# Order of the product pairs, queue of the gate stores, spread of the first loads and buffers of branch B's results in a hybrid mLSTM and differential-attention block

## Chip, cores and metric

One Trainium2 chip, one core of it. The metric is the device time of one execution in microseconds (us), less is better. Time before: median 1725.19 us of three runs (1722.07 to 1732.42).

## The reference, cut to what matters

S = D = 1024, batch 1, one layer, float32. The input is normalised, projected by `w_in` into twelve segments, and goes through two branches: A is an mLSTM with four heads of 256 in both directions over chunks of 128, behind a convolution of width five on its q and k; B is differential attention with eight heads (two score maps of 64 channels each, values of 128). Both results are projected, weighed with sigmoid gates, added, projected again and added to the input.

```python
h = rmsnorm(x, norm_g[layer])
proj = jnp.einsum('bsd,de->bse', h, w_in[layer])
(a_q, a_k, a_v, a_o, a_z, a_g, b_q, b_k, b_v, b_z, g_a, g_b) = jnp.split(
    proj, _split_points(), axis=-1)
...
hm = rmsnorm((h_fw + h_bw).transpose(0, 2, 1, 3), ml_norm_g[layer])
...
y_a = hm * jax.nn.sigmoid(a_o) * jax.nn.silu(a_z)
...
att = diff_attention(dq, dk, da_v, lam)
...
y_b = att.reshape(B, S, DA_WIDTH).astype(x.dtype) * jax.nn.silu(b_z)
...
mix = (jax.nn.sigmoid(g_a + gb[0]) * jnp.einsum('bsc,cd->bsd', y_a, w_branch_a[layer])
       + jax.nn.sigmoid(g_b + gb[1]) * jnp.einsum('bsc,cd->bsd', y_b, w_branch_b[layer]))
x = x + jnp.einsum('bsd,de->bse', mix, w_out[layer])
```

## The kernel before, in words

Every float32 product is made of three products in a rounded float32 form: each operand is split into a high part H and the low rest L, and H·H, L·H and H·L are added in PSUM. ScalarE casts the high parts, VectorE or GpSimd (POOL) subtracts for the low ones.

The program is a list of small units, each a few matmuls with what belongs to them, put in order by hand in `build` (L1572). `add` appends units; `weave` mixes two lists by their costs and by when a unit can be ready, so that one list fills the gaps of another. The order of TensorE (PE) is the order of this list (`keep(E.PE)`, L1671). The other engines, SyncE (SP) with its DMA queue among them, get their order from a scheduler that works with modelled times. Every engine executes in order: an instruction that waits holds back all behind it.

The stages, with their times in the profile:

1. Opening, 0 to 68 us: norm, transposes of the input, first z projections.
2. Product pairs, 68 to 490: the branch A segments of `w_in`. Two blocks of 128 columns are handled as a pair and multiplied in seven products in place of eight. `pairs` (L1617 on) lists sixteen narrow pairs (the pairs of k, q, o and z; `pair_units` L335, matmuls of 128x512 at L356) and then two wide pairs, the values (`wide_units` L375, seven products of 48 matmuls of 128x256 at L401). Within a pair the products run in the order 0, 3, 1, 4, 2, and 6 and 5 come interleaved with the next pair. The weight form of a product is made by `load_form` (L294) or `load_wide_form` (L258): sums or differences of the raw weight pieces on POOL (L264, L279), the cast on ScalarE (L287), the low part on VectorE for products 0, 4 and 6 and on POOL for the others (L288). A wide pair has four raw pieces of 128x4x256. Two go to `raw` tiles with the pair (`load_piece`, L246), and the two far ones to slots of the tag `big` (`kit`, six slots which the narrow pairs' results use too), through `spare` and `far_pieces`, called inside the last narrow pair's units (L1687 and L1688 of `build`). The sinks of the pairs convolve (L500 to L512), apply o and z, or store the values (L436).
3. Differential attention, 490 to 1148: per head and per block of queries scores (L1069), exponentials (L1074), transposes (L132), products with the values (L1105). Between them gate projections (`gate_units`, L960), the next heads' q, k and z projections (L558, L580) and values (`da_v`, L1038) serve as filler. `da_v(0)`, the values of heads 0 and 1, runs wholly ahead of head 0.
4. mLSTM, 1148 to 1425: `ml_units` (L1383) writes the order. For head n: `k` (L1186, L1225) and `v` (L1205) load and weigh chunks, `gb` (L1197) loads gate rows for the weight matrices W (L1280, L1282), `HL` (L1192) loads split k and q, `state` updates the matrix memories, `S` starts the scores. Nine gate projections are filler. A gate's `done` (L964) runs tanh on ScalarE into the tile `gt`, which has one buffer, and stores it (L967).
5. Rest of the gates and the passes through the branches' weights, 1425 to 1630: `load_y` (L1453) loads 128x1024 rows of a branch result into `yraw` (L1455, two buffers), casts on ScalarE (L1457), subtracts on VectorE (L1458). Branch B's eight (`yb`) come first.
6. Output projection and last norm, 1630 to 1724. The output weights (L1509) and squares (L1548) use the tag `yraw` too.

Of the kernel before, what the change touches and what calls it, by code (L numbers as in the profile page):

```python
# [7 lines left out]
F32 = mybir.dt.float32  # L8
# [6 lines left out]
S = 1024  # L15
D = 1024
# [4 lines left out]
NC = S // L  # L21
# [89 lines left out]
class Block:  # L111
# [110 lines left out]
    def pair_raws(self, p):  # L222
# [25 lines left out]
    def spare(self, n):  # L248
        while len(self.kit) < n:
            self.kit.append(self.big("kit")[:, 0:S])  # L250

    def far_pieces(self, p, blocks=(1, 0)):
        i = 0 if p % 2 == 0 else 4
        for b in blocks:
            self.praws[p][b][1] = self.kit[i + 1 - b].rearrange("p (k e) -> p k e", e=256)
            self.load_piece(p, b, 1)

    def load_wide_form(self, key):  # L258
        _, p, f = key
        a, g = self.a, self.p  # L260
        self.pair_raws(p)
        r1, r2 = self.praws[p]
# [697 lines left out]
    def gate_units(self, seg, i):  # L960
# [3 lines left out]
        def done(half, ps):  # L964
            t = self.wpool.tile([128, 512], F32, name="gt", tag="gt")
            self.a.activation(out=t, in_=ps, func=AF.Tanh, scale=0.5, bias=self.gbh[:, idx:idx + 1])  # L966
            (self.a if self.opening else self.q).dma_start(out=self.tg[seg][i][:, half * 512:(half + 1) * 512], in_=t)  # L967
# [415 lines left out]
    def ml_units(self, heads, gates):  # L1383
# [6 lines left out]
        for c in (3, 2, 1, 0):  # L1390
            un += x["k"](c) + x["v"](c)
        for c in range(NC):
            un += x["gb"](c) + x["HL"](c)
        un += take(8) + x["weigh"](3, 1) + take(3) + x["state"](3, 1)
        un += x["weigh"](2, 1) + take(5) + x["state"](2, 1)
        un += x["weigh"](1, 1) + take(4) + x["state"](1, 1) + x["split"](0)
        un += take(4) + x["S"](0)
        prev = None
        for n, x in enumerate(heads):
# [5 lines left out]
            for t in range(8):  # L1405
# [35 lines left out]
                if prev and t in (0, 2):  # L1441
                    un += prev["g"](t // 2)
                if nx:
# [9 lines left out]
    def load_y(self, src, i, slot):  # L1453
        raw = self.wy.tile([128, S], F32, name="yraw", tag="yraw", bufs=2)
# [45 lines left out]
    def load_wo(self, k, st, which):  # L1500
# [5 lines left out]
        else:  # L1506
            raw = self.wy.tile([128, D], F32, name="yraw", tag="yraw", bufs=2)
# [7 lines left out]
    def out_units(self, st):  # L1515
# [14 lines left out]
        def piece(t, i, g):  # L1530
# [16 lines left out]
            sq = self.wy.tile([128, D], F32, name="sqo", tag="yraw", bufs=2)  # L1547
# [24 lines left out]
    def build(self):  # L1572
# [21 lines left out]
        with pool(name="const", bufs=1) as self.const, \  # L1594
# [22 lines left out]
            self.pairs, sinks, self.praws, self.f, self.kit = [], [], {}, {}, []  # L1617
            for n in range(NH_A):
# [54 lines left out]
            w.add(do(lambda: setattr(self, "opening", False)), leave("p0"), enter("s0", "s0", side="right"), *g3)  # L1673
# [11 lines left out]
            fv = self.first_v  # L1685
# [13 lines left out]
            w.add(do(lambda: setattr(self, "ahead", True)), *qk[0], *z[0], *self.da_v(0, sts[0:2]))  # L1699
            prev = None  # L1700
            for h in range(NH_B):
# [7 lines left out]
                else:  # L1709
                    nxt = z[h - 1] + ahead + fill(FILL[h]) + z[h] if h else ahead + fill(FILL[0])  # L1710
# [82 lines left out]
```

## Time and profile before

| what | value |
|---|---|
| median of three runs | 1725.19 us (1722.07 to 1732.42) |
| profiled execution, its own time | 1725.98 us |
| its span in the trace | 1724.2 us |
| mean granted TensorE clock | 0.984 |
| busy: PE, VectorE (DVE), ScalarE (ACT), POOL | 1653.9, 1015.4, 776.8, 661.2 us |
| bytes on SP's and ACT's hardware queue | 196.03 MB |

The span leaves out 1.8 us of the profiled execution's time, before its first and behind its last recorded instruction. In the views, a row of the waits names the waiting instruction, its releaser, the total, the number of times and the longest; a row of the timeline has start, duration, engine, line, operation, output and inputs, and in brackets the idle time ahead of it with what ended it; a row of the windows has the stretch, its length, the busy time of each engine with the number of instructions, the granted clock, the share of the DMA engines and GB/s. SPq is SP as it issues DMAs; the time beside it is the issue, not the transfer.

### The profile page before, as it was taken

Reading aid. Unit: us, or ns where it says so; the run is one execution under the profiler, and the core shown is the slowest. Engines: PE = TensorE matmul, PEld = TensorE weight load, DVE = VectorE, ACT = ScalarE, POOL = GpSimd, SP = SyncE. Lnnn points to the kernel's source line nnn. Section 1 sums busy time; section 2 is a strip of 40 time slices with the busy share of each in tenths; the row PEclk is TensorE's granted clock in tenths of the full one; section 3 lists DMA queues with packets and bytes.
Section 4 is the critical chain, followed back from the end, with each engine's and each line's share of the span. In section 5 each row is a group of like instructions: output and inputs, shape, how many; then the busy total and the mean of one; then the engine's idle time right before and its main releaser. Section 6 shows DMA issues by size and latency. Waiting matters only on the chain. (4 is left out here: it accounts for less than half of the span.)

```text
span 1724.2 us, 25403 instructions
## 1 busy us (share of the span) xinstructions
PE 1653.9 (96%) x9335; PEld 1385.9 (80%) x9335; DVE 1015.4 (59%) x1817; ACT 776.8 (45%) x1548; POOL 661.2 (38%) x713
## 2 busy tenths in 40 slices
PE   7999999997999999999999999996999998999998
PEld 6777887877988788878878887785988876888887
DVE  5687678773324866777676676512666663226533
ACT  6455555553322545554554545523566653122221
POOL 4767766665342452533435152122232221222000
PEclk9999999998999999999999999998999998999999
DMA  5343434344252313212132231148777527444222
GB/s 182 94 134 115 147 110 135 110 153 128 111 172 61 86 37 86 70 38 79 48 88 54 58 86 38 50 144 227 225 217 201 154 81 243 134 145 136 86 86 86
DMA packets 191248, 199.77 MB, mean 116 GB/s; under 512 B 13466, under 2 KB 144883, under 8 KB 191123
## 3 DMA queue, kind: packets, MB, share of 16 engines
q1 hardware_dynamic: 189922, 196.03, 37.7%
q10 hardware_dynamic: 1200, 2.11, 0.3%
q8 instruction: 73, 1.20, 0.3%
q14 instruction: 53, 0.43, 0.1%
HBM read 124.60 MB, written 56.72 MB: 105 GB/s over the span
## 5 line engine op out<-in xcount | busy, mean ns | idle before, releaser
L558 PE MATMUL pj<-hH,wH 128*128 128x512 f32 x640 | 270.0, 422 | 13.9 <-ACT gt L966 11.9
L558 PE MATMUL pj<-hH,wL 128*128 128x512 f32 x640 | 253.3, 396 | 1.4 <-POOL wL L210 1.4
L558 PE MATMUL pj<-hL,wH 128*128 128x512 f32 x640 | 252.5, 394 | 0.0
L1074 ACT ACTIVATE e<-S,nm 128x1024 f32<-128x1024 f32 x128 | 142.5, 1115 | 98.0 <-DVE nm L1072 97.9
L212 POOL TENSOR_TENSOR wL<-raw,wH 128x1024 fp32r<-128x1024 f32 x34 | 82.7, 2433 | 235.4 <-ACT wH L207 235.4
L558 PEld LDWEIGHTS pj<-hH,wH 128*128 128x128 f32 x640 | 122.3, 191 | 47.3 <-issue 14.6
L1072 DVE TENSOR_REDUCE nm<-S 128x1 f32<-128x1024 f32 x128 | 150.6, 1218 | 13.6 <-PE S L1069 13.0
L558 PEld LDWEIGHTS pj<-hH,wL 128*128 128x128 f32 x640 | 121.5, 190 | 30.7 <-POOL wL L210 3.2
L558 PEld LDWEIGHTS pj<-hL,wH 128*128 128x128 f32 x640 | 122.2, 191 | 17.2 <-DVE hL L709 0.2
L558 PE MATMUL pj<-sl_yb,wH 128*128 128x512 f32 x384 | 122.1, 397 | 6.8 <-ACT sl_yb L1457 4.7
L1094 DVE TENSOR_TENSOR pL<-T,pH 128x512 fp32r<-128x512 f32 x128 | 87.2, 688 | 70.0 <-ACT pH L1093 68.6
L1093 ACT CAST pH<-T 128x512 fp32r<-128x512 f32 x128 | 75.1, 587 | 79.9 <-PE T L132 78.3
L1069 PE MATMUL S<-kst,qq 64*128 64x512 f32 x768 | 107.9, 411 | 1.7 <-ACT e L1074 1.7
L207 ACT CAST wH<-raw 128x1024 fp32r<-128x1024 f32 x48 | 50.4, 1051 | 107.0 <-PE pj L558 89.8
L558 PEld LDWEIGHTS pj<-sl_yb,wH 128*128 128x128 f32 x384 | 73.2, 191 | 25.8 <-ACT sl_yb L1457 6.2
L1080 DVE SCALAR_TENSOR_TENSOR e<-e,r,e 128x1024 f32<-128x1024 f32 x64 | 91.2, 1425 | 2.2
L1069 PEld LDWEIGHTS S<-kst,qq 64*128 64x128 f32 x768 | 68.5, 186 | 27.1 <-issue 11.4
L356 PE MATMUL T<-TH,wH 128*128 128x512 f32 x256 | 86.9, 398 | 1.1 <-ACT u L363 1.1
L502 DVE SCALAR_TENSOR_TENSOR pj<-cin,cols,pj 128x512 f32<-128x512 f32 x128 | 87.1, 747 | 1.1 <-ACT pj L500 1.1
L356 PE MATMUL T<-TH,wL 128*128 128x512 f32 x256 | 86.2, 398 | 1.4 <-ACT u L363 1.1
L132 PE MATMUL T<-ident,e 128*128 128x128 f32 x512 | 77.0, 273 | 5.4 <-ACT att L1107 3.5
L580 PE MATMUL pj<-wH,hH 128*128 128x256 f32 x256 | 75.8, 296 | 3.1 <-DVE hl L1002 2.2
(398 smaller groups left out, 4414.8 us busy)
## 6 DMA issues: line engine op xcount, KB each, us to landing
raw<-in_w_in_dram SPq DMA_DIRECT2D x84, 512.0 KB, 4.2
kst<-hl SPq DMA_DIRECT2D x64, 128.0 KB, 2.4
qq<-hl SPq DMA_DIRECT2D x64, 128.0 KB, 2.4
x<-in_x_dram SPq DMA_DIRECT2D x8, 512.0 KB, 6.4
cak<-y SPq DMA_DIRECT2D x16, 256.0 KB, 2.3
cakH<-cin SPq DMA_DIRECT2D x16, 256.0 KB, 4.4
cakL<-tz SPq DMA_DIRECT2D x16, 256.0 KB, 4.5
gm<-oz SPq DMA_DIRECT2D x16, 256.0 KB, 2.6
```

Source lines behind the costliest of these rows:

```text
L132: self.t.transpose(out, in_, self.ident[0:k, 0:k])
L212: self.p.tensor_tensor(out=wL, in0=raw, in1=wHf, op=ALU.subtract)
L356: self.t.matmul(ps, lhsT=l[:, k, :], rhs=r[:, k, :], start=(first and k == 0 and m == 0), stop=(k == 3 and m == 2), skip_group_check=not f ...
L502: v.scalar_tensor_tensor(out=acc, in0=raw[:, o + x:o + x + 512], scalar=w(x), in1=acc, op0=ALU.mult, op1=ALU.add)
L558: self.t.matmul(ps, lhsT=l[:, k, :], rhs=r, start=(n == 0), stop=(n == 23))
L580: self.t.matmul(ps[:, i, :], lhsT=l, rhs=r[:, k, :], start=(kh == 0 and k == 0 and m == 0), stop=(kh == 1 and k == 3 and m == 2))
L1069: self.t.matmul(ps[:, o], lhsT=qq[r, x, c], rhs=k[r, y, o], start=(m == 0), stop=(m == 2))
L1072: v.tensor_reduce(out=nm, in_=ps, axis=AX.X, op=ALU.max, negate=True)
L1074: a.activation(out=e, in_=ps, func=AF.Exp, bias=nm[:, 0:1], accum_out=Z[:, j, t:t + 1])
L1080: v.scalar_tensor_tensor(out=e0, in0=e, scalar=r[:, 0:1], in1=e0, op0=ALU.mult, op1=ALU.add)
L1093: a.copy(pH[:, :, s], ps)
L1094: v.tensor_tensor(out=pL[:, :, s], in0=ps, in1=pH[:, :, s].bitcast(F32), op=ALU.subtract)
```

## The change

1. The wide pairs are the first two of `pairs`. All six slots of `big` are allocated as `kit` as soon as the pool exists, all four pieces of a wide pair are loaded at once, and both pairs' pieces with the first form. `spare` and `far_pieces` are gone.
2. While the flag `ml` is set (stage 4), a gate's store is issued by ScalarE, which made the tile, and not by SP. 19 stores move, 13 stay.
3. The first mLSTM head's loads are spread: k and v of chunks 3, 2, 1 first, the others between the state updates, the last two of `gb` and `HL` inside head 0.
4. `yraw` has four buffers.
5. `da_v(0)` is cut: 20 of its units stay ahead of head 0, the other twelve are woven into it as filler.

```diff
@@ pair_raws
-            if p > self.first_v + 1:
-                self.far_pieces(p)
+            for b in (1, 0):
+                self.praws[p][b][1] = self.kit[(0, 4)[p % 2] + 1 - b].rearrange("p (k e) -> p k e", e=256)
+                self.load_piece(p, b, 1)
@@
-    def spare(self, n):
-        while len(self.kit) < n:
-            self.kit.append(self.big("kit")[:, 0:S])
-
-    def far_pieces(self, p, blocks=(1, 0)):
-        i = 0 if p % 2 == 0 else 4
-        for b in blocks:
-            self.praws[p][b][1] = self.kit[i + 1 - b].rearrange("p (k e) -> p k e", e=256)
-            self.load_piece(p, b, 1)
@@ load_wide_form
         self.pair_raws(p)
+        if p == 0:
+            self.pair_raws(1)
@@ gate_units, done
-            (self.a if self.opening else self.q).dma_start(out=self.tg[seg][i][:, half * 512:(half + 1) * 512], in_=t)
+            (self.a if self.opening or self.ml else self.q).dma_start(out=self.tg[seg][i][:, half * 512:(half + 1) * 512], in_=t)
@@ ml_units
-        for c in (3, 2, 1, 0):
+        hl = lambda x, c: x["gb"](c) + x["HL"](c)
+        for c in (3, 2, 1):
             un += x["k"](c) + x["v"](c)
-        for c in range(NC):
-            un += x["gb"](c) + x["HL"](c)
-        un += take(8) + x["weigh"](3, 1) + take(3) + x["state"](3, 1)
-        un += x["weigh"](2, 1) + take(5) + x["state"](2, 1)
-        un += x["weigh"](1, 1) + take(4) + x["state"](1, 1) + x["split"](0)
+        un += take(8) + x["weigh"](3, 1) + take(3) + x["state"](3, 1) + hl(x, 0)
+        un += x["weigh"](2, 1) + take(5) + x["state"](2, 1) + x["k"](0) + x["v"](0)
+        un += x["weigh"](1, 1) + take(4) + x["state"](1, 1) + x["split"](0) + hl(x, 1)
         un += take(4) + x["S"](0)
@@
+                if n == 0 and t in (0, 2):
+                    un += hl(x, 2 + t // 2)
@@ load_y, load_wo, out_units
-        raw = self.wy.tile([128, S], F32, name="yraw", tag="yraw", bufs=2)
+        raw = self.wy.tile([128, S], F32, name="yraw", tag="yraw", bufs=4)
...
@@ build
+            for g in range(2):
+                self.pairs.append(("v", "av", g))
+                sinks.append(self.v_sink(g))
             for n in range(NH_A):
...
-            self.first_v = len(self.pairs)
-            for g in range(2):
-                self.pairs.append(("v", "av", g))
-                sinks.append(self.v_sink(g))
@@
+            w.add(do(lambda: self.kit.extend(self.big("kit")[:, 0:S] for _ in range(6))), *g3)
@@
-            products = [(self.pair_units if i < fv else self.wide_units)(i, sinks[i]) for i in range(len(self.pairs))]
-            products[fv - 1][2].insert(0, do(lambda: (self.spare(5), self.far_pieces(fv))))
-            products[fv - 1][5].append(do(lambda: (self.spare(6), self.far_pieces(fv + 1))))
+            products = [(self.pair_units if i >= 2 else self.wide_units)(i, sinks[i]) for i in range(len(self.pairs))]
@@
-            w.add(do(lambda: setattr(self, "ahead", True)), *qk[0], *z[0], *self.da_v(0, sts[0:2]))
+            w.add(do(lambda: setattr(self, "ahead", True)), *qk[0], *z[0])
+            v0 = self.da_v(0, sts[0:2])
+            w.add(*v0[:20])
@@
-                    nxt = z[h - 1] + ahead + fill(FILL[h]) + z[h] if h else ahead + fill(FILL[0])
+                    nxt = z[h - 1] + ahead + fill(FILL[h]) + z[h] if h else v0[20:] + ahead + fill(FILL[0])
```

In the changed file most lines stand seven lower: its L960 is the store of L967, its L1449 the load of L1455, its L257, L272 and L281 the operations of L264, L279 and L288.

What this does to the order on the engines, at three places. First POOL at the start of the product pairs, in the changed kernel (s and kit hold sums of raw pieces, wL is a low part, f a tile of the opening):

```order
26 L676 TENSOR_TENSOR f<-f,t_684 128x512
27 L272 TENSOR_TENSOR s_772<-raw,kit 128x1024
28 L281 TENSOR_TENSOR wL<-s_772,wH 128x1024
29 L257 TENSOR_TENSOR kit<-s_772,raw 128x1024
30 L257 TENSOR_TENSOR s_945<-raw 128x1024
31 L281 TENSOR_TENSOR wL<-kit,wH 128x1024
32 L257 TENSOR_TENSOR kit<-kit 128x1024
33 L472 MEMSET cin 128x2
34 L473 MEMSET cin 128x2
35 L281 TENSOR_TENSOR wL<-s_945,wH 128x1024
36 L272 TENSOR_TENSOR s_1198<-raw,kit 128x1024
```

These operations stood near the end of the product pairs before; they now follow the opening's last work on POOL, and the forms of the narrow pairs follow them.

Second, SP at the mLSTM's first loads and ScalarE at its gate stores. Before, SP (akf, akH, akL, aqH, aqL are loads of k and q, gb of gate rows, tgb the gate's store):

```order
337 L1192 DMA aqL<-caqL_139 128x256
338 L1197 DMA gb<-gg 128x256 x2
339 L1192 DMA akH<-cakH_114 128x256
340 L1192 DMA akH<-cakH_115 128x256
341 L1192 DMA akL<-cakL_122 128x256
342 L1192 DMA akL<-cakL_123 128x256
343 L1192 DMA aqH<-caqH_130 128x256
344 L1192 DMA aqH<-caqH_131 128x256
345 L1192 DMA aqL<-caqL_138 128x256
346 L1192 DMA aqL<-caqL_139 128x256
347 L967 DMA tgb_79<-gt 128x512
348 L174 DMA raw<-in_w_in_dram 128x8x128
```

In the changed kernel the same store is on ScalarE. The rows show what each waits for; DMAHW0 to DMAHW7 are eight counters that all transfers of SP and ScalarE use in turn:

```order
850 L959 ACTIVATE gt<-pj,gbh 128x512 [waits DMAHW6_49,PE_49,Activation_49]
851 L1218 ACTIVATE kwH<-T,gc_ws 128x256 [waits PE_49]
852 L960 DMA tgb_79<-gt 128x512 [waits DMAHW5_49,Activation_49]
853 L1218 ACTIVATE kwH<-T,gc_ws 128x256 [waits DVE_49]
854 L1215 COPY kn<-T 128x512 [waits PE_49]
855 L1218 ACTIVATE kwH<-T,gc_ws 128x256 [waits DVE_49] x2
856 L1275 ACTIVATE W_11597<-W_11597,gc_negM 128x128 [waits Pool_49]
857 L1275 ACTIVATE W_11646<-W_11646,gc_negM 128x256 [waits Pool_49]
858 L1275 ACTIVATE W_11603<-W_11603,gc_negM 128x256 [waits Pool_49]
859 L1275 ACTIVATE W_11652<-W_11652,gc_negM 128x128 [waits Pool_49]
860 L207 CAST wH<-raw 128x1024 [waits DMAHW0_49,PE_49]
861 L959 ACTIVATE gt<-pj,gbh 128x512 [waits DMAHW5_49,PE_49]
```

The store of one tanh (row 852) stood on SP behind all four chunks' loads; it now stands on ScalarE right behind its tanh and one other activation, waits on a counter itself, and the casts and the four exponentials of W stand behind it.

Third, SP at branch B's results. Before:

```order
562 L967 DMA tga_72<-gt 128x512
563 L1455 DMA yraw<-yb_90 128x1024
564 L1455 DMA yraw<-yb_91 128x1024
565 L1470 DMA tgl<-tgb_74 128x1024
566 L1470 DMA tgl<-tgb_75 128x1024
567 L1455 DMA yraw<-yb_92 128x1024
568 L967 DMA tga_72<-gt 128x512
569 L1455 DMA yraw<-yb_93 128x1024
```

In the changed kernel:

```order
542 L1449 DMA yraw<-yb_90 128x1024
543 L1449 DMA yraw<-yb_91 128x1024
544 L1449 DMA yraw<-yb_92 128x1024
545 L1449 DMA yraw<-yb_93 128x1024
546 L960 DMA tga_72<-gt 128x512
547 L1449 DMA yraw<-yb_94 128x1024
548 L1449 DMA yraw<-yb_95 128x1024
549 L960 DMA tga_73<-gt 128x512
550 L1449 DMA yraw<-yb_96 128x1024
551 L1449 DMA yraw<-yb_97 128x1024
```

The first gate store of this stage went to ScalarE, four loads stand together, and only single gate stores stand between the others; the loads of the gates (tgl) come behind the last of them.

More of the change, by code (lines that the diff above doesn't have):

```diff
@@ L1506, in load_wo @@
         else:
-            raw = self.wy.tile([128, D], F32, name="yraw", tag="yraw", bufs=2)
+            raw = self.wy.tile([128, D], F32, name="yraw", tag="yraw", bufs=4)
             h, l = self.slot(which), self.slot(which)
@@ L1546, in piece @@
             v.tensor_tensor(out=x[:, c], in0=ps, in1=x[:, c], op=ALU.add)
-            sq = self.wy.tile([128, D], F32, name="sqo", tag="yraw", bufs=2)
+            sq = self.wy.tile([128, D], F32, name="sqo", tag="yraw", bufs=4)
             a.activation(out=sq[:, c], in_=x[:, c], func=AF.Square, accum_out=ssq[:, i:i + 1])
```

3 lines of the change are left out of this document (1 added, 2 removed).

## The prediction

> **What bounds the kernel now.** The first look goes to the page's busy times.
>
> ```profile
> PE 1653.9 (96%) x9335; PEld 1385.9 (80%) x9335; DVE 1015.4 (59%) x1817; ACT 776.8 (45%) x1548; POOL 661.2 (38%) x713
> ```
>
> TensorE (PE) is busy for 1653.9 of 1724.2 us; no other engine passes 59%. The change leaves TensorE's matmuls as they are, so it can win only what TensorE loses: some 70 us of idle time, and time at a reduced granted clock behind the longer gaps. The second look is the waits of TensorE: who ended them, total, times, longest.
>
> ```profile
> PE pj L558 <- ACT gt L966: 11.9, 1, 11.9
> PE pj L558 <- ACT sl_yb L1457: 4.7, 3, 2.8
> PE T L401 <- DVE wL L288: 3.5, 1, 3.5
> PE T L128 <- ACT kwH L1225: 3.4, 4, 2.8
> PE T L401 <- POOL wL L288: 3.1, 1, 3.1
> PE T L401 <- ACT wH L287: 2.6, 1, 2.6
> ```
>
> They fall into three places that the change touches: L401 is the wide value products, L966 a gate's tanh in the mLSTM, L1457 the loads of branch B. The third look is the table of windows at each place (stretch, length, busy us of PE, PEld, DVE, ACT and POOL, granted clock, DMA share, GB/s). I count two losses: idle is 5.00 minus PE's busy time, clock loss is busy time times one minus the clock.
>
> Place A, the wide products:
>
> ```profile
> 390.00:395.00 5.00, 1.54 (x12) 1.25 (x11) 4.33 (x7) 2.55 (x5) 1.95 (x1) 1.00 0.15 54
> 395.00:400.00 5.00, 5.00 (x32) 5.00 (x31) 2.71 (x4) 2.15 (x4) 1.78 (x2) 0.66 0.71 194
> 400.00:405.00 5.00, 4.24 (x25) 3.35 (x23) 0.00 (x0) 0.59 (x1) 1.61 (x1) 1.00 1.06 360
> 405.00:410.00 5.00, 0.51 (x2) 0.30 (x2) 0.00 (x0) 2.85 (x4) 4.92 (x3) 0.93 0.07 23
> 410.00:415.00 5.00, 4.48 (x21) 4.48 (x22) 1.38 (x2) 1.19 (x2) 5.00 (x4) 0.50 0.00 0
> 415.00:420.00 5.00, 5.00 (x34) 4.75 (x34) 1.12 (x1) 1.05 (x1) 3.72 (x2) 0.89 0.47 114
> 420.00:425.00 5.00, 5.00 (x40) 4.76 (x39) 1.50 (x3) 1.17 (x2) 3.36 (x2) 1.00 0.95 304
> ```
>
> Idle 3.46 + 0.76 + 4.49 + 0.52 = 9.2 us; clock 1.7 + 2.2 + 0.6 = 4.5 us (full speed is back in the last row). A loses **13.7 us**. Place B, the start of the mLSTM:
>
> ```profile
> 1170.00:1175.00 5.00, 2.31 (x11) 2.01 (x12) 1.37 (x3) 1.56 (x4) 1.92 (x6) 0.89 0.62 203
> 1175.00:1180.00 5.00, 4.34 (x17) 3.36 (x16) 1.39 (x6) 0.62 (x1) 0.00 (x0) 0.77 0.75 157
> 1180.00:1185.00 5.00, 0.00 (x0) 0.00 (x0) 0.02 (x2) 0.00 (x0) 0.00 (x0) 0.91 0.71 224
> 1185.00:1190.00 5.00, 0.00 (x0) 0.00 (x0) 0.00 (x0) 0.00 (x0) 0.00 (x0) 0.50 0.90 288
> 1190.00:1195.00 5.00, 3.74 (x11) 3.04 (x12) 0.00 (x0) 0.69 (x1) 0.00 (x0) 0.57 0.94 290
> ```
>
> Idle 2.69 + 0.66 + 5 + 5 + 1.26 = 14.6; clock 0.25 + 1.0 + 1.6 = 2.9; together **17.5 us**. Place C, branch B's first pass:
>
> ```profile
> 1445.00:1450.00 5.00, 2.65 (x10) 1.33 (x8) 1.33 (x2) 2.58 (x3) 2.34 (x1) 1.00 0.72 215
> 1450.00:1455.00 5.00, 1.96 (x3) 0.74 (x3) 1.23 (x1) 0.74 (x2) 0.00 (x0) 0.53 0.78 275
> 1455.00:1460.00 5.00, 3.98 (x9) 2.61 (x9) 3.07 (x3) 1.55 (x2) 0.00 (x0) 0.50 0.41 132
> ```
>
> Idle 6.4, clock 2.9: **9.3 us**. Place E, the end of the attention's first head, which the waits show only in pieces:
>
> ```profile
> 585.00:590.00 5.00, 3.72 (x24) 2.26 (x23) 4.97 (x6) 3.47 (x9) 4.50 (x3) 1.00 0.30 70
> 590.00:595.00 5.00, 4.40 (x18) 3.28 (x18) 4.08 (x6) 1.62 (x4) 0.00 (x0) 0.52 0.62 143
> 595.00:600.00 5.00, 4.97 (x33) 4.49 (x34) 3.01 (x5) 3.45 (x7) 0.44 (x2) 0.80 0.00 0
> ```
>
> Idle 1.9, clock 3.1: **5.0 us**. The four places hold 45.5 us; a change that cured them at no cost would end at 1680.
>
> B's clock loss has a rule beside it. The Trainium skill, "TensorE: Matmul & The Clock Gate", Part 1 (the HAM clock gate), says that the clock drops to half after an idle window of about 3.4 us and returns after about 3.4 us of sustained work. By that rule one gap costs at most half of 3.4 us, 1.7 us as an estimate, where the rows of B give 2.9 (two gaps, and slow work between them); the sum below would be about a microsecond smaller by it. The rows decide.
>
> **The change part by part.** *The wide pairs first.* Why A stalls stands in SP's and POOL's rows of the timeline (start, duration, engine, line, operation; in brackets the idle time before it):
>
> ```profile
> 397.42 5.18 SPq L246 DMA_DIRECT2D kit<-in_w_in_dram  x3
> 403.39 2.35 POOL L279 TENSOR_TENSOR s<-raw,kit 128x1024 f32<-128x1024 f32 x1 [6.43 <-issue]
> 410.42 2.37 POOL L288 TENSOR_TENSOR wL<-kit,wH 128x1024 fp32r<-128x1024 f32 x1
> ```
>
> The far pieces are asked for only when the last narrow pair frees their slots; then POOL needs four operations of 2.35 us in a row before the third form is there. The change issues them in the opening, so all of the 13.7 us goes. What it puts in its place is the same chain at 62 us, and here are its rows of today:
>
> ```profile
> 65.82 1.70 POOL L319 TENSOR_TENSOR s<-raw 128x512 f32<-128x512 f32 x1 [0.83 <-DMA raw<-in_w_in_dram]
> 71.58 0.73 PE L356 MATMUL T<-TH,wL 128*128 128x512 f32 x2 [0.33 <-POOL wL L329]
> raw<-in_w_in_dram SPq DMA_DIRECT2D x84, 512.0 KB, 4.2
> ```
>
> Now seven pieces of 512 KB follow one another from about 62.1 us. If they land in order, the second raw and the first far piece are there at about 67 (one piece takes 4.2 us): POOL adds until 69.4, ScalarE casts, POOL has the low half at about 72.8. TensorE starts at 67.9 and needs for 48 matmuls about 6.0 us (40 in 5 us, last row of A), so it asks at 73.9: no stall. The next form costs POOL three more operations, until 79.9, just when it is wanted. If the seven share the bandwidth evenly, they land only at 72.7 (3.67 MB at the 360 GB/s of A's third row), and the first stall is about 5 us, with its clock 6. Bounds 0 and 6; I take **+2**, nearer the first, because one queue issues them in turn.
>
> The narrow pairs now end the stage. The attention's first rope tiles wait there for stores of the last pair's results, which in the new order stand behind a weight load that waits for POOL. The nearest row is the stall that the rope has already:
>
> ```profile
> 521.32 0.39 PE L580 MATMUL pj<-wH,hH 128*128 128x256 f32 x1 [2.16 <-DVE hl L1002]
> ```
>
> Bounds 0 (the store is out by then) and 5 (twice this wait with its clock); I take **+2.5**. A's net is −13.7 + 4.5 = **−9.2**.
>
> *Twelve of the first value units moved into head 0.* They are 60 of the 192 matmuls of 128x256, so head 0 gets some 7.5 us more filler (8 matmuls per us), where today the weave runs dry and TensorE waits for ScalarE. It covers E's 1.9 us of idle time and with that its clock. The first score product then comes 7.5 us earlier in the order and may find its operands barely loaded, which can give back what is won: bounds −5 and 0. I take **−4.5**, because the wide value products no longer fill SP's queue ahead of these loads.
>
> *Gate stores on ScalarE's queue, first loads spread.* B's rows:
>
> ```profile
> 1156.45 0.69 ACT L966 ACTIVATE gt<-pj,gbh 128x512 f32<-128x512 f32 x1 [4.04 <-PE pj L558]
> 1185.50 1.71 SPq L1192 DMA_DIRECT2D aqL<-caqL  x2
> 1187.38 0.32 SPq L967 DMA_DIRECT2D tgb<-gt  x1
> 1190.52 0.69 ACT L966 ACTIVATE gt<-pj,gbh 128x512 f32<-128x512 f32 x1 [14.78 <-DMA tgb<-gt]
> ```
>
> The tanh ended at 1157.1 and its store was issued at 1187.4, 30 us later, behind the loads of the first head; the tile has one buffer, so the next tanh waited, and with it the PSUM bank and TensorE. A store on ScalarE's own queue goes out behind its tanh. I let TensorE keep the waits for kwH (3.4 us, second fence: a chain of load, selection and exponential that the change doesn't shorten) and 0.6 for gate weights that POOL now makes behind four selections: of 17.5 us, 4 stay, **−13.5**. Bounds −17.5 and 0.
>
> The new price: in the new order each of the 19 stores on ScalarE waits, besides for its tanh, for the transfer that used the same one of eight counters before it, and all of ScalarE's later casts and exponentials stand behind that. The issue takes 0.32 us (row of 1187.38), 6.1 in all, and ScalarE is busy for 45%. A transfer eight issues back has mostly landed: at about 0.6 us per issue it is 4.8 us old, and a load takes about 4.2. Bounds 0 and 8; I take **+2**.
>
> *Four yraw buffers.* C's queue:
>
> ```profile
> 1428.19 0.32 SPq L967 DMA_DIRECT2D tga<-gt  x1
> 1428.61 0.88 SPq L1455 DMA_DIRECT2D yraw<-yb  x2
> 1441.20 4.25 SPq L1455 DMA_DIRECT2D yraw<-yb  x2
> 1448.46 3.36 SPq L1455 DMA_DIRECT2D yraw<-yb  x2
> ```
>
> Two loads fit; each next one waits until ScalarE and VectorE have split a slot, and the last two go out at 1448 to 1452, with TensorE waiting since about 1446.5. With four slots, and the gate store no longer ahead of them, four go out together, no later than 1428.6. The seventh then needs the slot that today lets the fifth go, so the last two go out at about 1441.2; they land about 4 us later and are split 2 us after that, at about 1447.2, against about 1446.5 when TensorE runs dry (C's first row holds half a stretch of work). So 0.7 to 0.8 stays; I take 0.8: **−8.5**; bounds −9.3 and −4 (the last two held up at SP behind a tgl load or a store that waits).
>
> The same slots serve the output weights and the squares at the end. The waits of TensorE name nothing there, so I cost that at nothing: the products of the branches cover those loads, and without that cover one would cost a landing of 4.2 us.
>
> **The sum:** −9.2 − 4.5 − 13.5 + 2 − 8.5 = −33.7 us. The profiled execution took 1725.98 (1724.2 of span), 0.8 above the median of 1725.19: 1725.98 − 33.7 − 0.8 = 1691.5, said as **1692 us**.
>
> **The rivals.** *The stall of A only moves to the opening.* For it: the same POOL chain, seven transfers at once, and POOL busy until 65 with opening work. Against it: 3.5 of A's idle time was VectorE's backlog of convolution work, which the opening has not. A keeps 13.7 instead of 2: 1692 + 11.7 = **1704**.
>
> *B's stall stays.* ScalarE's store waits for a counter whose last user is a load that SP issues late, and the gate stops as before. For it: DMA share 0.90 and 0.94 in B's last rows, and 3.1 us from the store's issue to the next tanh. Against it: the loads are spread, so the store's counter belongs to the first chunk's. Then 1692 + 13.5 = **1705.5**. The Trainium skill, "DMA: Bandwidth & Descriptors", section "Issuing engines are not separate DMA queues", speaks for this one: issuing from several engines saves only the sequencer's time to issue, which it calls small. The rows above disagree in this case: that time, with its waits, was 30 us for one store.
>
> *ScalarE is held at every gate: slower.* Place: the 19 stores between 1150 and 1425. If each waits for a landing of 3.1 us (1187.38 to 1190.52, one store) and TensorE meets it whole, because the exponentials of the weights are next on ScalarE, the price is 19 x 3.1 = 59 us in place of 2: 1692 + 57 = **1749**. It decides from 1.9 us per store on (35.7 / 19). Against it: ScalarE has over half of its time free.
>
> *C stays:* the loads are bound by SP, which stops at stores and slots. Then 1692 + 8.5 = **1700**.
>
> **How the numbers follow.** Forecast 0.64, A moves 0.12, B stays 0.11, C stays 0.08, ScalarE held 0.05. All but the last lie under 1708 with their middle, not with their tails (B and A together give 1717). The bound of one per cent, about what a measurement of this kernel can tell from no change, is 17 us: faster by more 0.82, within it 0.13, slower 0.05. The range: below, everything cured with no new cost is 1680, and 2 us more for waits not counted; above, the two likeliest rivals in part: 1678 to 1714.
>
> **What would show it.** In the changed profile TensorE's wait for gt should be gone, and no window at about 1185 with no PE work; if ScalarE shows idle time before casts while TensorE waits for W or kwH, the third rival holds. L401 should run at 68 to 150 us with waits under 3 us; a wait for POOL wL of over 5 us there is the first rival. At 585 to 600 the windows should show 5.00 at a clock of 1.00, and the waits for sl_yb should be under 1.5 us. The prediction is wrong if TensorE's idle time still sums to over 55 us, or if a new wait stands at the rope above 5 us.

## The result, and the profile after

The changed kernel takes 1704.68 us (median of four runs, 1701.42 to 1706.29) against 1726.86 us before: a ratio of 0.9868, with a 95% interval of 0.9833 to 0.9903. That is 22 us less where 34 were forecast: inside the range, on the right side of one per cent (the interval ends just short of it), and 13 us above the predicted time. The profiled execution took 1703.18 us, with a span of 1701.1 and a mean granted clock of 0.993.

TensorE's busy time, from the page after:

```profile
PE 1644.1 (97%) x9335; PEld 1379.2 (81%) x9335; DVE 1025.1 (60%) x1817; ACT 775.9 (46%) x1548; POOL 660.0 (39%) x713
```

The same 9335 matmuls; that they are busy for 10 us less is the clock: counted in windows of 2 us over the whole span, the lost clock cost 18.8 us before and 8.8 after. TensorE's idle time fell from 70.3 to 57.0 us. The waits of TensorE after (releaser, total, times, longest) say where the rest is:

```profile
PE T L394 <- DVE tz L427: 7.5, 1, 7.5
PE T L132 <- DMA gin<-in_gate_b_dram: 5.2, 1, 5.2
PE T L132 <- ACT W L1320: 4.8, 6, 1.6
...
PE pj L551 <- DVE sl_yb L1452: 2.9, 2, 2.1
...
PE T L394 <- POOL wL L281: 1.9, 1, 1.9
...
PE T L128 <- ACT kwH L1218: 0.6, 3, 0.2
```

The wait of 11.9 us for gt is gone, and so are the three waits of the wide products. In their place stands a wait that the list before did not have: 7.5 us of the wide products for tz, an operation of VectorE; and the waits for W (L1320) have grown from 1.9 to 4.8 us. L394, L427, L551, L1320 and L1452 are the L401, L434, L558, L1327 and L1458 of the kernel before.

To see which stage gave what I use five instructions as milestones, each the first or last matmul of a line. Their rows after (the two times at the end are the starts of the first and of the last):

```profile
L573 PE MATMUL pj<-wH,hH x256: 276/283/419, 508.4 to 965.0; 128*128 128x256 f32 x128
L1062 PE MATMUL S<-kst,qq x768: 383/393/504, 528.2 to 1097.7; 64*128 64x512 f32 x192
L128 PE MATMUL T<-vH,kwH x96: 276/284/419, 1149.3 to 1381.4; 128*128 128x258 f32 x96
L128 PE MATMUL PO<-vH,WH x64: 274/282/387, 1177.4 to 1398.2; 128*128 128x256 f32 x64
L1536 PE MATMUL pj<-sl_yb,sl_r x153: 278/389/389, 1606.4 to 1691.9; 128*128 128x512 f32 x135, 128*128 128x256 f32 x18
```

L573, the L580 of before, is the matmul of the attention's values (`v_units`); stage 3 above lists it with the q, k and z projections, and head 0's stand ahead of it. "Products" is from the start to the first of these value products (508.4), "attention" on to the last score product (1097.7), "mLSTM" from the first state update (1149.3) to its last product (1398.2), "passes" on to the first output product (1606.4). The same lines of every other kernel below give the table, in us:

| kernel | products | attention | mLSTM | passes | span |
|---|---|---|---|---|---|
| before | 513.2 | 593.9 | 255.3 | 215.5 | 1724.2 |
| changed | 508.4 | 589.3 | 248.9 | 208.2 | 1701.1 |
| changed, gate chain later (first try) | 502.6 | 588.1 | 249.3 | 210.3 | 1696.7 |
| changed, gate stores on SP | 508.2 | 589.0 | 240.8 | 206.9 | 1691.5 |
| changed, first loads ahead | 509.9 | 588.3 | 251.7 | 210.6 | 1706.9 |
| changed, two yraw buffers | 508.7 | 589.6 | 248.3 | 216.2 | 1709.3 |
| changed, first values all ahead | 509.5 | 594.8 | 248.6 | 209.6 | 1708.9 |
| changed, wide pairs last | 512.2 | 589.5 | 249.2 | 208.8 | 1706.0 |
| changed, POOL's operations halved | 506.9 | 589.6 | 247.5 | 207.9 | 1698.2 |
| before, spread loads alone | 511.9 | 593.4 | 238.9 | 214.1 | 1705.0 |
| changed, chain later and stores on SP | 499.4 | 587.9 | 237.2 | 207.4 | 1678.6 |

The kernel with the stores' move alone is missing here: its profiled execution ran at a granted clock of 0.75 and took 2027 us, so of this kernel only the times of its eleven undisturbed runs are used.

The change gave 4.8 us in the products, 4.6 in the attention, 6.4 in the mLSTM and 7.3 in the passes; these are the 23 us. Forecast were, in the same order, 9.2, 4.5, 11.5 and 8.5. Two stages lie about five short each: products and mLSTM.

**The products.** The windows after at the new wait (stretch, length, busy us of PE, PEld, DVE, ACT, POOL, granted clock, DMA share, GB/s):

```profile
120.00:125.00 5.00, 0.88 (x8) 0.68 (x6) 4.79 (x5) 2.21 (x4) 4.05 (x3) 1.00 0.58 158
125.00:130.00 5.00, 1.62 (x7) 1.63 (x8) 4.84 (x9) 0.00 (x0) 1.75 (x1) 0.54 0.50 156
130.00:135.00 5.00, 5.00 (x36) 5.00 (x35) 2.16 (x5) 1.05 (x1) 0.00 (x0) 0.78 0.03 8
```

Idle 7.5 us and 1.9 us of clock: 9.4 us lost while VectorE is busy throughout. What it does there, with POOL beside it and the matmul that waits, in the timeline after (start, duration, engine, line, operation):

```profile
116.58 2.04 DVE L846 TENSOR_SCALAR gch<-gch 64x256 f32<-64x256 f32 x1
119.11 1.99 DVE L848 TENSOR_SCALAR gch<-gch 64x256 f32<-64x256 f32 x1 [0.48 <-ACT gch L847]
121.13 0.42 DVE L849 TENSOR_TENSOR gch<-gch 64x256 f32<-64x256 f32 x1
121.65 0.42 DVE L852 TENSOR_TENSOR gch<-gch 64x256 f32<-64x256 f32 x1
122.10 2.44 DVE L853 TENSOR_TENSOR gch<-gch 64x256 f32<-64x256 f32 x1
124.58 2.44 DVE L855 SCALAR_TENSOR_TENSOR gch<-gch 64x256 f32<-64x256 f32 x1
127.06 0.68 DVE L861 TENSOR_TENSOR_SCAN gch<-gch 32x256 f32<-32x256 f32 x1
127.67 0.65 DVE L427 TENSOR_TENSOR tz<-T,tz 128x512 fp32r<-128x512 f32 x1
```

```profile
121.81 2.45 POOL L281 TENSOR_TENSOR wL<-kit,wH 128x1024 fp32r<-128x1024 f32 x1 [0.87 <-ACT wH L280]
124.35 2.40 POOL L257 TENSOR_TENSOR kit<-kit 128x1024 f32<-128x1024 f32 x1
```

```profile
128.38 0.58 PE L394 MATMUL T<-wH,TH 128*128 128x256 f32 x1 [7.50 <-DVE tz L427]
```

gch is the gate chain of the mLSTM: the log-sigmoids and running sums of its gate rows, put by `build` at fixed places in the sequence of pairs (its projection at pair 1). At pair 1 stood a narrow pair; now the second wide pair stands there. On VectorE the chain got ahead of the subtraction of tz that frees the bank for the next wide product. The two operations at 122.10 and 124.58 end 0.3 us after POOL's two (124.26 and 126.75); a `TENSOR_TENSOR` of the same form takes 0.42 us at 121.13, when POOL has nothing to do.

**The attention.** At the end of head 0, the prediction's place E, the windows after:

```profile
585.00:590.00 5.00, 3.18 (x24) 2.76 (x23) 3.60 (x5) 3.73 (x7) 5.00 (x5) 1.00 0.31 70
590.00:595.00 5.00, 5.00 (x25) 3.88 (x25) 2.38 (x4) 0.00 (x0) 2.54 (x3) 1.00 0.45 104
```

The lost clock, 3.1 us before, is gone. The idle time is not: from 580 to 600 it is 1.8 us where it was 3.0.

**The mLSTM.** Its start is cured as forecast: from the first state update to 1177.4 it loses 3.9 us where it lost 17.8. The rest loses more than before: from 1177.4 on TensorE is idle for 10.2 us, where the same stretch before had 6.1. ScalarE and the matmul that waits for it, after:

```profile
1207.76 0.69 ACT L959 ACTIVATE gt<-pj,gbh 128x512 f32<-128x512 f32 x1
1208.33 0.63 ACT L1252 CAST CH<-C 128x516 fp32r<-128x516 f32 x1
1212.22 0.33 ACTq L960 DMA_DIRECT2D tgb<-gt  x1
1212.60 0.39 ACT L1347 ACTIVATE PO<-hm 128x256 f32<-128x256 f32 x1 [3.63 <-DMA gb<-gg]
```

```profile
1213.56 0.71 PE L132 MATMUL T<-ident,W 128*128 128x128 f32 x2 [1.57 <-ACT W L1320]
```

The tanh ends at 1208.45 and its store is issued at 1212.22. One cast stands between them, until 1208.96. A store waits for nothing but its tanh and a counter (the rows in the section on the change), and the trace names the transfer of gb as what ended ScalarE's wait; the scaling of W stands behind it. Four of the 19 stores were issued so late after their tanh's end, by 2.0, 3.8, 1.8 and 2.8 us, 10.4 us together, with such a cast of some 0.5 us in three of them. That the other three waited for a counter too is concluded from the order; the trace names other releasers for the instructions behind them. A fifth store, 2.0 us late at 1403.76, stood behind an activation that waited for VectorE.

**The passes.** The yraw loads go out together as forecast, but the last low part is late:

```profile
1430.46 1.23 DVE L1452 TENSOR_TENSOR sl_yb<-yraw,sl_yb 128x1024 fp32r<-128x1024 f32 x1 [0.89 <-ACT sl_yb L1451]
1432.93 2.59 DVE L1452 TENSOR_TENSOR sl_yb<-yraw,sl_yb 128x1024 fp32r<-128x1024 f32 x1 [1.24 <-ACT sl_yb L1451]
```

```profile
1432.08 2.36 POOL L212 TENSOR_TENSOR wL<-raw,wH 128x1024 fp32r<-128x1024 f32 x1 [9.94 <-ACT wH L207]
```

```profile
1435.57 0.50 PE L551 MATMUL pj<-sl_yb,wH 128*128 128x512 f32 x1 [2.12 <-DVE sl_yb L1452]
```

It took 2.59 us beside POOL's subtraction, twice its 1.23, and TensorE waited 2.1 us for it. In the kernel before, one of these low parts took 2.63 us beside POOL as well, at 1436.21, where TensorE did not wait for it.

### The profile page after: what moved, and what is told of

Its sections match the earlier page's. It is cut to its first block, busy times and chain, and to the rows that moved or that the text cites. A ratio compares the mean times of both kernels' runs of the same rounds, so it can differ in the third digit from the quotient of the medians.

```text
span 1701.1 us, 25404 instructions
## 1 busy us (share of the span) xinstructions
PE 1644.1 (97%) x9335; PEld 1379.2 (81%) x9335; DVE 1025.1 (60%) x1817; ACT 775.9 (46%) x1548; POOL 660.0 (39%) x713
## 5 line engine op out<-in xcount | busy, mean ns | idle before, releaser
L551 PE MATMUL pj<-hH,wH 128*128 128x512 f32 x640 | 268.4, 419 | 1.9 <-ACT f L664 1.5
L551 PE MATMUL pj<-hH,wL 128*128 128x512 f32 x640 | 252.4, 394 | 1.6 <-POOL wL L210 1.6
L551 PE MATMUL pj<-hL,wH 128*128 128x512 f32 x640 | 251.3, 393 | 0.2 <-DVE hL L702 0.2
L551 PEld LDWEIGHTS pj<-hH,wH 128*128 128x128 f32 x640 | 121.4, 190 | 33.4 <-issue 13.1
L551 PEld LDWEIGHTS pj<-hH,wL 128*128 128x128 f32 x640 | 120.6, 188 | 31.0 <-POOL wL L210 3.6
L551 PEld LDWEIGHTS pj<-hL,wH 128*128 128x128 f32 x640 | 121.4, 190 | 17.6 <-DVE hL L702 0.6
L551 PE MATMUL pj<-sl_yb,wH 128*128 128x512 f32 x384 | 120.3, 394 | 3.4 <-DVE sl_yb L1452 2.9
L551 PEld LDWEIGHTS pj<-sl_yb,wH 128*128 128x128 f32 x384 | 72.8, 190 | 20.1 <-DVE sl_yb L1452 3.5
L1273 POOL TENSOR_SCALAR_AFFINE_SELECT W<-gb 128x128 f32<-128x128 f32 (+1 forms) x64 | 22.7, 357 | 144.4 <-DVE W L1322 94.1
```

The costliest lines, as they stand in the source:

```text
L551: self.t.matmul(ps, lhsT=l[:, k, :], rhs=r, start=(n == 0), stop=(n == 23))
```

## The experiments

My theory after the result: (1) the first edit lost half of its gain to the gate chain on VectorE; (2) the stores' move to ScalarE is no part of the cure but a cost, since the spread of the loads cures the long stall alone; (3) the yraw buffers and the split values are worth what was forecast. The rivals are in the expectations. All ratios are against the kernel before; the changed kernel's 0.9868 corresponds to 1700.5 us where the kernel before took 1723.3. The interval of that ratio reaches 6 us to each side, so a difference of a few us from 1700.5 is read together with the stages in the table.

### The gate chain two pairs later

```diff
-            more = {(1, 0): gl + gmm}
-            for (i, k), step, un in (((2, 6), 1, rows[:6]), ((4, 6), 2, rows[6:]), ((6, 6), 2, chain), ((6, 13), 1, ang[:1]),
-                                     ((8, 4), 2, weights), ((8, 13), 1, ang[1:2]), ((10, 4), 2, ang[2:7]), ((10, 5), 2, columns),
+            more = {(3, 0): gl + gmm}
+            for (i, k), step, un in (((4, 6), 1, rows[:6]), ((6, 6), 2, rows[6:]), ((8, 6), 2, chain), ((6, 13), 1, ang[:1]),
+                                     ((10, 4), 2, weights), ((8, 13), 1, ang[1:2]), ((10, 4), 2, ang[2:7]), ((12, 5), 2, columns),
```

> The changed kernel with the mLSTM's gate chain two pairs later (its projection from pair 1 to pair 3, the row operations, the chain, the weights and the columns likewise), so that it meets narrow pairs again. Theory: the new stall of 7.5 us at 121 us is VectorE working through this chain ahead of the subtraction that frees the wide product's bank; with the chain gone from there, 7.5 us of waiting and some 1.9 us of clock go: 9 us less than the changed kernel, about 1695 us. Rival: the wide pair stalls by itself (late stores, late pieces), or the chain stops the narrow pairs as it stopped the wide one: no change, 1704 us. If the theory holds, the chain's 64x256 operations should take about 1.3 us beside the narrow pairs' 128x512 subtractions on POOL, as they did before the change, and not 2.4.

Measured: 1694.47 us, ratio 0.9826 (0.9805 to 0.9848). The wait for tz is gone, and beside narrow pairs the chain's operations take 1.40 us (L853 and L855), not 2.44. But the stage gained 5.8 us and not 9.4, because another wait came. Its waits of TensorE in the products:

```profile
PE T L349 <- ACT u L356: 5.1, 3, 3.4
PE T L394 <- POOL wL L281: 1.8, 1, 1.8
```

The later weights of the chain now met the angles' sine at 326 us on ScalarE: loading the table (1.28 us) and waiting for VectorE's part of the sine (4.20 us) held up the copy u, and TensorE waited 3.4 us. So the chain is the cause of the 7.5 us, and its later parts have a place that matters too.

### The gate stores back on SP

```diff
-            (self.a if self.opening or self.ml else self.q).dma_start(out=self.tg[seg][i][:, half * 512:(half + 1) * 512], in_=t)
+            (self.a if self.opening else self.q).dma_start(out=self.tg[seg][i][:, half * 512:(half + 1) * 512], in_=t)
```

> The changed kernel with the mLSTM's gate stores back on SP's queue; the loads stay spread. Theory: a store on ScalarE holds ScalarE until the transfer that used its counter before has landed, up to 3.6 us, and this costs the mLSTM about 5 us between 1177 and 1398 us; the spread loads alone cure the long stall at the start: 2 to 5 us less than the changed kernel, 1700 to 1703 us, and TensorE's waits for W at L1320 fall from 4.8 to about 2 us. Rival: the queue cured the start; then the wait for gt returns, 5 to 12 us more, 1710 to 1717 us.

Measured: 1693.32 us, ratio 0.9824 (0.9811 to 0.9838): more than expected, some 7 us below the changed kernel. The mLSTM takes 240.8 us in place of 248.9, no wait for gt came back, and its waits for W are those of the kernel before:

```profile
PE T L132 <- ACT W L1320: 1.9, 3, 0.7
```

The stores' move to ScalarE costs 8 us in the mLSTM once the loads are spread. The same matmuls between the milestones are busy for 236.4 us in the changed kernel and 233.0 here, and TensorE's idle time is 12.5 and 7.8 us: 4.7 of the 8 are waits, of which W has 2.9.

### The first loads ahead again, stores on ScalarE

```diff
-        for c in (3, 2, 1):
+        for c in (3, 2, 1, 0):
             un += x["k"](c) + x["v"](c)
+        for c in range(NC):
+            un += x["gb"](c) + x["HL"](c)
...
```

> The changed kernel with the first mLSTM head's loads all ahead again, as before the change; the gate stores stay on ScalarE. Theory: each of the two edits by itself frees the store from the 62 loads, so the long stall stays away; what comes is later tiles behind the loads: 0 to 4 us more than the changed kernel, 1704 to 1709 us. Rival: the stores on ScalarE wait for the counters of loads that SP issues late, and the stall of 12 us is back on ScalarE: 1715 to 1720 us.

Measured: 1701.94 us, ratio 0.9881 (0.9865 to 0.9897), mLSTM 251.7 us: the long stall stays away, as the theory had it. The loads' order is worth 2.8 us of the mLSTM while the stores are on ScalarE, in a profiled execution that was the slowest of its five; the time, 1.4 us above the changed kernel's, does not resolve it.

### Each of the two alone, on the kernel before

The first takes the edit to the loads alone, the second the edit to the stores alone.

```diff
+        hl = lambda x, c: x["gb"](c) + x["HL"](c)
...
+        un += take(8) + x["weigh"](3, 1) + take(3) + x["state"](3, 1) + hl(x, 0)
...
```

> The kernel before with one edit alone: the first mLSTM head's loads spread. The gate stores stay on SP. Theory: the spread is what cures the long stall, and the stores' move to ScalarE adds nothing to that: some 14 us less than before (mLSTM from 255 to about 241 us between its first state update and its last product), 1709 us. Rival: the cure needs both edits: 0 to 7 us less, 1716 to 1723 us.

Measured: 1706.62 us, ratio 0.9894 (0.9879 to 0.9909), 17 us less than before, mLSTM 238.9 us in place of 255.3. The spread alone gives 16.4 us in the mLSTM; it needs no help.

```diff
-            (self.a if self.opening else self.q).dma_start(out=self.tg[seg][i][:, half * 512:(half + 1) * 512], in_=t)
+            (self.a if self.opening or self.ml else self.q).dma_start(out=self.tg[seg][i][:, half * 512:(half + 1) * 512], in_=t)
```

> The kernel before with one edit alone: the mLSTM's gate stores on ScalarE's queue, all first loads still ahead. Theory: the stall of 11.9 us behind the loads goes, and ScalarE's waits for the transfers' counters give most of it back (the stores cost about 8 us): 3 to 6 us less than before, 1718 us. Rival: the stores pay by themselves as forecast, 10 us or more less, 1713 us or below; or the counters belong to loads that come late, and nothing is won.

Measured: 1719.52 us, ratio 0.9975 (0.9963 to 0.9987), 4 us less than before, as the theory had it; that the stall went and ScalarE's waits came in its place is not shown. So from the kernel before, the spread alone gives 16.4 us in the mLSTM, and the changed kernel with both edits 6.4.

### POOL's operations cut in halves

```diff
+        def both(e, out, x, y, op):
+            for k in (0, 2):
+                e.tensor_tensor(out=out[:, k:k + 2], in0=x[:, k:k + 2], in1=y[:, k:k + 2], op=op)
+        sub = lambda out, x, y: both(g, out, x, y, ALU.subtract)
```

> The changed kernel with each of the wide pairs' sums and differences on POOL cut into two of 128x512; nothing else. It is to tell what makes the gate chain on VectorE so long. Theory: an operation of VectorE that starts beside one of POOL ends only with it (64x256 operations took 0.42 us alone and 2.44 beside a POOL operation of 2.40 us). With halves of about 1.3 us each the chain's four long operations should take about 1.3 to 1.4 us, so the stall at 121 us falls from 7.5 to 3 or 4 us, and the time by 3 to 5 us to about 1697 us (1700 to 1701 on this chip for the changed kernel). Rival: the length is the chain's own: the operations stay at 2.0 to 2.4 us, the stall at 7 to 8, the time within 1 us.

Measured: 1701.7 us, ratio 0.9867 (0.9847 to 0.9886), no change in the time. The chain on VectorE and TensorE's wait (lines moved by six):

```profile
118.97 1.47 DVE L855 TENSOR_TENSOR gch<-gch 64x256 f32<-64x256 f32 x1
120.55 1.31 DVE L858 TENSOR_TENSOR gch<-gch 64x256 f32<-64x256 f32 x1
121.90 1.37 DVE L859 TENSOR_TENSOR gch<-gch 64x256 f32<-64x256 f32 x1
123.30 1.37 DVE L861 SCALAR_TENSOR_TENSOR gch<-gch 64x256 f32<-64x256 f32 x1
```

```profile
PE T L400 <- DVE tz L433: 5.9, 1, 5.9
```

The two long operations fell from 2.44 to 1.37 us, so their length is POOL's and not their own. But the two that had found POOL idle (0.42 us) now took 1.47 and 1.31, and the stall fell only by 1.6 us, not by the 3 to 4 expected. The time does not resolve that.

### Two yraw buffers, and the first values all ahead

The first puts `bufs=2` back in the three places.

> The changed kernel with two buffers for branch B's results again, as before the change. Theory: the four buffers are worth what the time between the mLSTM's last product and the output's first shows, 215.5 before and 208.2 us after the change: 6 to 7 us more than the changed kernel, with the long wait of TensorE for sl_yb back at 2.8 us: 1707 us on this chip, where the changed kernel should take 1700.5 (its ratio of 0.9868 times 1723.3). Rival: the gate stores' move alone freed SP for these loads, and the buffers add nothing: 0 to 2 us.

Measured: 1710.32 us, ratio 0.9923 (0.9908 to 0.9938). The passes take 216.2 us in place of 208.2, 8.0 more (6 to 7 were expected), and TensorE waits for the casts again:

```profile
PE pj L551 <- ACT sl_yb L1451: 4.1, 3, 2.0
PE pj L551 <- DVE sl_yb L1452: 2.9, 6, 0.8
```

The second puts `w.add(*v0)` ahead of head 0.

> The changed kernel with all of the first values' units ahead of head 0 again. Theory: the twelve units fill the stall at the end of head 0, where the attention from its first projection to its last score lost 4.6 us (593.9 before, 589.3 after): 4 to 5 us more than the changed kernel, about 1705 us, and the windows at 10 to 25 us past the head's end show a clock near 0.5 again. Rival: the stall went because the product stage ended in another way (other stores in flight): no change.

Measured: 1707.79 us, ratio 0.9905 (0.9888 to 0.9922). The attention takes 594.8 us, 5.5 more (4 to 5 were expected), with the stall and the low clock back at the end of head 0:

```profile
585.00:590.00 5.00, 3.32 (x14) 2.01 (x12) 4.05 (x7) 2.74 (x6) 1.12 (x1) 0.72 0.87 201
590.00:595.00 5.00, 5.00 (x27) 4.83 (x27) 3.60 (x5) 2.40 (x4) 0.44 (x2) 0.60 0.03 6
```

Both theories hold.

### The wide pairs last

This is the changed kernel with the first edit undone whole.

> The changed kernel with the wide pairs last and their far pieces late, as before the change; everything else as changed. From the two traces the first edit is worth 4.8 us up to the attention's first projection (2.9 in the product stage, 1.9 at the rope) of the 13.7 us that its stall had cost. Theory: the parts add up, 5 us more than the changed kernel, 1709 us. Rival: the later stages hide part of it or depend on it (other addresses, other stores in flight): 1704 us, or 1718 us where the whole 13.7 us is back.

Measured: 1706.88 us, ratio 0.9901 (0.9888 to 0.9915). The products take 512.2 us, 3.8 more than in the changed kernel, and the three waits of the wide products are back. The time is 6 us above the changed kernel's, where 5 were expected: the parts add up.

### Both repairs

```diff
-            (self.a if self.opening or self.ml else self.q).dma_start(out=self.tg[seg][i][:, half * 512:(half + 1) * 512], in_=t)
+            (self.a if self.opening else self.q).dma_start(out=self.tg[seg][i][:, half * 512:(half + 1) * 512], in_=t)
...
-            more = {(1, 0): gl + gmm}
-            for (i, k), step, un in (((2, 6), 1, rows[:6]), ((4, 6), 2, rows[6:]), ((6, 6), 2, chain), ((6, 13), 1, ang[:1]),
+            more = {(3, 0): gl + gmm}
+            for (i, k), step, un in (((4, 6), 1, rows[:6]), ((5, 6), 2, rows[6:]), ((6, 6), 2, chain), ((6, 13), 1, ang[:1]),
```

> Two repairs in one on the changed kernel: the gate stores back on SP's queue (worth 7 to 8 us when made alone), and the gate projection and its first row operations two pairs later, the rest of the row operations one pair later; weights and columns keep their places, so that they don't meet the angles' sine as they did in the earlier try (a new wait of 3.4 us at a narrow pair, which gave back a part of the 7.5). If the two are independent and the collision was what gave it back: 1693 less 8, about 1685 us. If the narrow pairs pay for the chain wherever it stands: 1688 to 1690 us.

Measured: 1684.0 us, ratio 0.9763 (0.9745 to 0.9781): 40 us less than before and some 17 less than the changed kernel. Its waits of TensorE in the products:

```profile
PE T L349 <- ACT u L356: 2.9, 4, 1.1
PE T L394 <- POOL wL L281: 1.8, 1, 1.8
PE T L394 <- DVE tz L427: 0.3, 1, 0.3
```

The products take 499.4 us, 9.0 less than in the changed kernel: nearly the whole of the stall and its clock, and with the later parts of the chain in their old places the wait of 3.4 us does not come. The mLSTM takes 237.2.

## Why the prediction was right, and where its terms were off

**A, −9.2 forecast, −4.8 measured.** The step "all of the 13.7 us goes" held: the three old waits are gone. The start, taken as +2 from a range of 0 to 6, cost one wait for POOL's wL of 1.9 us; POOL's first sum began at 67.30, near the 67 of pieces that land in turn and not the 72.7 of pieces that share the bandwidth. The end, +2.5 taken, cost nothing: from the last matmul of the pairs to the attention's first value product it took 21.8 us in place of 23.7, and the rope's wait for hl is 2.2 us in both kernels. The step that failed is "what it puts in its place is the same chain at 62 us". The chain of weights on POOL was not all that came to stand there: the gate chain, whose place is counted in pairs, came to lie in a wide pair, and cost 9.4 us. POOL had a part in it, but through VectorE, whose operations beside it took 2.44 us and not 0.42. I had priced POOL and the queue and not asked what else is tied to a pair's number. The order of VectorE's instructions would have told: it shows the chain ahead of the subtraction of tz.

**E, −4.5 forecast, −4.6 measured,** and 5.5 when undone alone. The size came out, the reason in part: the filler was to cover the idle time and with that the clock, but what went is the clock and only 1.2 us of the idle time. The filler was miscounted too: twelve units of six matmuls are 72 of the 192, 9 us and not 7.5.

**The mLSTM, −13.5 + 2 forecast, −6.4 measured.** The first term holds in place and size: 4 us were to stay at the start, 3.9 do. Its reason was half wrong. I gave the cure to both edits together; the spread alone brings 16.4 us, the stores alone 4 us of run time. The mis-sized term is the price of ScalarE's waits for counters: +2 from a range of 0 to 8, where the stores cost 8.1 (248.9 less 240.8). "A transfer eight issues back has mostly landed" fits 15 of the 19 stores; four others go out 1.8 to 3.8 us after their tanh, and in the case shown the scaling of W is next behind, on TensorE's path. The third rival described this mechanism with the right place and named the point from which it decides, 1.9 us per store; the stores cost 0.4 each, so the change stayed on the faster side.

The Trainium skill, "DMA: Bandwidth & Descriptors", section "Issuing engines are not separate DMA queues", says that issuing from several engines saves only the time to issue, which is usually small. In this case the move won 4 us alone and cost 8 us of the mLSTM beside the spread loads; the cost comes from ScalarE's waits ahead of the issue, which is another reason than the section's. The same page, "Anatomy of one DMA — SWDGE (gpsimd) path", a section on transfers that GpSimd issues, says of DMAs that a wait for a semaphore takes place on the issuing sequencer before the dispatch; here, on ScalarE's queue, the 3.63 us ahead of the activation at 1212.60 agree.

**C, −8.5 forecast, −7.3 measured,** and 8.0 when undone alone. The residue at TensorE is 3.4 us and not 0.8; half of the surplus is the low part that took 2.59 us beside POOL in place of 1.23.

With the measured sizes the sum is −4.8 − 4.6 − 6.4 − 7.3 = −23.1, the change of the spans. The forecast had 10.6 us more: 4.4 in the products (a stall of 9.4 that no term had, against the rope's 2.5 that did not come and 1.9 won there; these make 5.0, and 0.6 is not placed), 5.1 in the mLSTM (a price of 8 taken as 2, against a cure larger by 1) and 1.2 in the passes.

**The signs and the rivals.** The wait for gt is gone and no new wait stands at the rope, as named. The other signs did not come as named: the wide products have a wait of 7.5 us where waits under 3 were named, the longest wait for sl_yb is 2.1 us and not under 1.5, the window from 585 to 590 holds 3.18 us of matmuls and not 5.00, and ScalarE idles ahead of its work while TensorE waits for W, the third rival's sign. TensorE's idle time, 57.0 us, is above the 55 that the prediction named as the point from which it is wrong: its sum cured too much, though the time lies inside its range. The measured time is the first rival's number, 1704, but that is chance: the wait for POOL's wL that the rival named as its sign, over 5 us, is 1.9, and more than half of what was missing lies in the mLSTM and the passes.

## What to carry to other kernels

Work that is placed by counting units of another work, as the gate chain is by pairs, moves when these units are reordered; before moving a stage, list what else is tied to its numbers and look at the order of every engine that the moved stage needs, not only of the one that made it wait. When a store holds up a queue, first make the queue short: spreading the loads alone gave 16.4 us in the mLSTM here, while moving the store gave ScalarE, which feeds TensorE, a wait that SP could afford. And undo each part of a change alone: here one of five cost 8 us, and without it and with the chain moved the kernel gains 40 us in place of 22.

## What the runs showed of the hardware

In these rows an operation of VectorE on two tensors in SBUF that started while one of POOL ran ended a fixed time after POOL's end, whatever POOL had left to do: 1.08 us for the low part of 128x1024 at 1432.93 (2.59 us in all, 1.23 alone), 0.55 us for a low part of 128x512 at 145.17 (1.68 in all, 0.68 alone), and 0.28 us for the 64x256 operations of the chain (2.44 in all, 0.42 alone). That is in each case its own time less some 0.15 us, so it did nearly all of its work behind POOL's end. With POOL's operations cut in halves the 64x256 operations took 1.31 to 1.47 us. One that started first was not held: the low part at 1443.88 in the kernel before took its 1.23 us, though POOL began at 1444.92. A subtraction that reads one operand from PSUM was not held either: the one at 140.47 took 0.69 us beside POOL's from 140.04 to 142.44, as at 137.49 with POOL idle.

The Trainium skill, "GPSIMD Engine Reference", section 1 (Specifications), says that POOL shares its SBUF interfaces with VectorE, with contention for instructions of VectorE in a 2-port performance mode or with two SBUF inputs. The operations with two tensors in SBUF agree with that, with these numbers. The two of the chain with one tensor and a constant, 2.0 us at 116.58 and 119.11, were stretched as well; whether they ran in such a mode no run here shows.
